# One product for the high and the low activations in the feature-major units of a one-core layer kernel

## The chip, the cores and the metric

The kernel runs on one core of a Trainium2 chip. The metric is the device time of one execution in microseconds; lower is better. The time before is 1656.69 us, the median of three runs (1654.15 to 1658.95).

A core has five engines that matter here, each with an instruction queue of its own that it works off in order: TensorE (PE in the profile; its weight loads are listed apart as PEld), VectorE (DVE), ScalarE (ACT), GpSimd (POOL) and SyncE (SP), which issues the weight transfers. They wait for each other by semaphores.

## The reference

One decoder layer on 256 tokens of width 2048, in float32:

```python
u = rmsnorm(h, w1)
qkv_A, z_A, b_A, a_A, q_B, k_B, v_B, g_B, gate_A, gate_B = split(u @ w_in)
q, k, v = silu(causal_conv(qkv_A, width 4))       # mixer A
o_A = gated_delta_rule(l2norm(q), l2norm(k), v, sigmoid(b_A), decay(a_A))
o_B = retention(rotary(q_B), rotary(k_B), v_B)    # mixer B
h = h + (sigmoid(gate_A) * o_A + sigmoid(gate_B) * o_B) @ w_out
h = h + SwiGLU(rmsnorm(h, w2))
return rmsnorm(h, wf)
```

Both mixers have 8 heads with 128 key and 256 value columns. The delta rule and the retention go by chunks of tokens.

## The kernel before

**Precision.** Float32 accuracy is had from TensorE's faster 32-bit type by splitting: a value is a high part (rounded to that type) and a low part (the rest). A product of two split values takes three products: high by high, high by low, low by high. The activations `u` are split once, into `uh` and `ul`. Each weight tile of 128 x 2048 is split when it arrives: ScalarE writes `hi` (L169), VectorE writes `lo` as raw minus `hi` (L170).

**Units.** The projections are cut into units of one weight tile. In a *feature-major* unit the weights are the stationary operand: 128 output features, 16 slices of 128 input features, 256 tokens as the moving columns. For each slice, PE multiplies `hi` with the high activations (L235) and then the same `hi` with the low ones (L236), each 128x256; when all slices are done come 16 products of `lo` with the high ones (L238). All 48 go into one half of a PSUM bank, 128x256. In a *token-major* unit the activations are stationary and the weights move, 512 columns at a time (L286, L287, L291); some of these are computed as Strassen sums of half tiles (`Z_t`, L378 to L382).

There are 64 feature-major units. Each of the four blocks (two heads each) has eight for the convolution of mixer A (k0, k1, q0, q1, v00, v01, v10, v11; functions `conv_unit`) and four for the rotary part of mixer B (r0 to r3; `rot_evac`); then 16 units multiply the merged mixers by `w_out` (`wo_evac`). After them the FFN runs; its products are token- or group-wise and are not feature-major.

**What follows a unit.** A convolution unit is read by VectorE from PSUM times `rstd_b` into `cb` (L501); ScalarE scales it by the first tap (L504); VectorE adds three taps (L506); ScalarE takes the sigmoid (L509); VectorE multiplies the two (L511) into `kT`, `qT` or `vt`. A rotary unit is read from PSUM by VectorE three times (L798 to L800) and summed into `rot` (L801). A `w_out` unit is added to `hT` by VectorE (L1096).

**Order.** Units follow lists written by hand; Strassen units are woven between the units of a block. `run_units` runs a unit and then what was put off to it: `after(n, fn)` runs `fn` when n more units have been issued. The weights run ahead of the units through 3 raw, 2 `hi` and 2 `lo` buffers. Within that program order a scheduler decides the order of each engine's queue. PSUM has eight banks: four for sums (which the first units also use), two for units (`pp`), two for everything else (`mx`); so with `pp` alone, a unit gets the bank of the unit two before it. In the first block, the function `decay` computes the decays from a small product `pab` through ScalarE's sigmoid, exp and log (L1012 to L1020), `gt` on VectorE (L1024) and two small PE products `pe` and `pd` (L1029 to L1040).

`ACT_TABLE_LOAD` in a row is ScalarE loading a table before a function that the loaded table lacks. Copies and scalings need none.

Of the kernel before, what the change touches and what calls it, by code (L numbers as in the profile page):

```python
# [66 lines left out]
def kernel(  # L67
# [156 lines left out]
            for fn in events.pop(done[0], []):  # L224
                fn()

    def feature_major(src, nk, ah, al, name, evac):
        o = []

        def begin():  # L230
            o.append(ps_unit(f"ps_{name}")[:, :S])

        def products(hi, lo, k0, k1):
            for k in range(k0, k1):
                PE.matmul(o[0], hi[:, k * P:(k + 1) * P], ah[:, k, :], start=(k == 0), stop=False)  # L235
                PE.matmul(o[0], hi[:, k * P:(k + 1) * P], al[:, k, :], start=False, stop=False)  # L236
            for k in range(k0, k1):
                PE.matmul(o[0], lo[:, k * P:(k + 1) * P], ah[:, k, :], start=False, stop=(k == nk - 1))  # L238

        def compute(hi, lo):  # L240
            begin()
            g = nk if unit[0] != 3 or not first[0] else nk // Q2
            for k in range(0, nk, g):
                products(hi, lo, k, k + g)
            evac(o[0])
        compute.steps = begin, products, lambda: evac(o[0])
        units.append((src, nk * P, name, compute))

    def start_pair(before):

        c = [units[i][3].steps for i in range(2)]
        for i in range(2):
            fetched.append(wtile("raw", units[i][2], F32))
            parts.append((wtile("hi", units[i][2]), wtile("lo", units[i][2])))
            loaded.append(parts[i])
        for q in range(4):
            before(q)
            r = slice(512 * q, 512 * q + 512)
            for i in range(2):
# [13 lines left out]
        units[1] = units[1][:3] + (both,)  # L273

    def token_major(src, uh, ul, name, evac, bank):
        pst = []
# [165 lines left out]
            PE.matmul(pb[:, c * P:(c + 1) * P], ones, dg[:, c], start=True, stop=True)  # L442
        return pb

    uh = act.tile([P, KT, S], F32R, tag="a0", name="uh")
    ul = act.tile([P, KT, S], F32R, tag="a1", name="ul")
    xs = act.tile([P, KT, S], F32, tag="a2", name="xs")
    xq = act.tile([P, KT, S], F32, tag="a3", name="xq")
    mm = {}
# [5 lines left out]
    def t1(name, n=S):  # L455
        return mixp.tile([P, 260], F32, tag="t1", name=name, bufs=T1B)[:, :n]
# [21 lines left out]
    def z_tiles(name):  # L478
        return mt([P, 5, S], "Z", f"Z_{name}"), t1(f"s1_{name}")

    def flat(t):
        return t.rearrange("p a b -> p (a b)")

    def v4(ps, n=P):
        return ps[:, :4 * n].rearrange("p (a b) -> p a b", a=4)

# [3 lines left out]
    def conv_unit(b, i, name, dst, then):  # L490

        def evac(o):
            if done[0] <= HOLD + 1:
                after(HOLD + 1 - done[0], lambda: finish(o))
            else:
                finish(o)

        def finish(o):
            cb = t1(f"cb_{name}", S + 3)
            G.memset(cb[:, 0:3], 0.0)  # L500
            V.tensor_tensor(out=cb[:, 3:], in0=o, in1=rstd_b, op=ALU.mult)  # L501
            cv = t1(f"cv_{name}")
            w = cvw[:, b * 8 + i]
            A_.activation(cv, cb[:, 0:S], AF.Copy, scale=w[:, 0:1])  # L504
            for j in range(1, 4):
                V.scalar_tensor_tensor(out=cv, in0=cb[:, j:j + S], scalar=w[:, j:j + 1], in1=cv,  # L506
                                       op0=ALU.mult, op1=ALU.add)
            sg = t1(f"sg_{name}")
            A_.activation(sg, cv, AF.Sigmoid)  # L509
            d = dst()  # L510
            V.tensor_tensor(out=d, in0=cv, in1=sg, op=ALU.mult)  # L511
            then(d)
        feature_major(wqk[b * 12 + i], KT, uh, ul, name, evac)

    def new_parts(i):

        mm[i] = act.tile([P, 2, KT // 2, S], F32R, tag=f"a{2 + i}", name=f"m{i}")

    def merged_parts(b, j):
        k = 4 * (b % 2) + 2 * j  # L520
        return flat(mm[b // 2][:, 0, k:k + 2]), flat(mm[b // 2][:, 1, k:k + 2])

    class Merged:
        def __init__(self, part):
            self.part = part

        def __getitem__(self, r):
            _, k, t = r
            return mm[k // (KT // 2)][:, self.part, k % (KT // 2), t]

    def split_rest():

        new_parts(1)
        if "wait" in mm:
            for j in range(2):
                hv, lv = merged_parts(2, j)
                w = mm["wait"][:, 512 * j:512 * j + 512]
# [20 lines left out]
    def block(b):  # L558
# [231 lines left out]


        def rot_evac(i):
            def evac(o):
                if i == 0:
                    T["rot"] = mt([P, 4, S], "rv", f"rot_{b}")
                ra = t1(f"ra_{b}_{i}")
                rb_ = t1(f"rb_{b}_{i}")
                V.tensor_tensor(out=ra, in0=o, in1=cosr, op=ALU.mult)  # L798
                V.tensor_tensor(out=rb_[0:64], in0=o[64:128], in1=sinr[64:128], op=ALU.mult)
                V.tensor_tensor(out=rb_[64:128], in0=o[0:64], in1=sinr[0:64], op=ALU.mult)  # L800
                V.tensor_tensor(out=T["rot"][:, i], in0=ra, in1=rb_, op=ALU.add)  # L801
# [87 lines left out]
        def merge(j):  # L889
# [163 lines left out]
    done[0] = unit[0] = 0  # L1053
    first[0] = False

    mh, ml = Merged(0), Merged(1)


    with tc.tile_pool(name="ffn", bufs=1) as ffn:
        for tag in WBUFS:  # L1060
# [9 lines left out]
        hh = act.tile([P, KT, S], F32R, tag="a0", name="hh")  # L1070
        hl = act.tile([P, KT, S], F32R, tag="a1", name="hl")
# [301 lines left out]
```

## Time and profile before

| | before |
|---|---|
| median of three runs | 1656.69 us |
| profiled execution | 1654.24 us |
| its span in the trace | 1652.5 us |
| PE busy | 1626.6 us, 98% |
| DVE busy | 1292.9 us, 78% |
| ACT busy | 821.6 us, 50% |
| chain that ended last | PE 91%, DVE 4%, DMA 3% |

The profile is one execution. Busy time counts the instructions of an engine; matmuls are pipelined, so the records of neighbouring ones overlap, and the pace of PE is read from start to start, not from a record's duration. The chain is followed back from the last instruction to what released each step.

### The profile page before, as it was taken

How to read it: one execution, taken by the hardware profiler on the slowest of the kernel's cores; microseconds unless marked ns; L12 is line 12 of the kernel's file. 1: busy time of each engine (PE TensorE's matmuls, PEld its weight loads, DVE VectorE, ACT ScalarE, POOL GpSimd, SP SyncE). 2: the span in 40 equal slices, each digit the busy share in tenths (PEclk: the TensorE clock that was granted, in tenths of full speed). 3: DMA queues.
4: the chain of work that ended last, by engine and by line, in shares of the span. 5: the costliest groups of instructions: out<-in, count | busy, mean ns of one | idle time of the engine just before them, and what ended most of it. 6: DMA issues, size and time to landing. Idle time of an engine off the chain costs nothing.

```text
span 1652.5 us, 26750 instructions
## 1 busy us (share of the span) xinstructions
PE 1626.6 (98%) x11226; PEld 1459.9 (88%) x11226; DVE 1292.9 (78%) x1648; ACT 821.6 (50%) x815; POOL 35.0 (2%) x64
## 2 busy tenths in 40 slices
PE   7999999999999999999999999999999999999998
PEld 6987899988998889988899888888888888888887
DVE  7797468887897878776766877889987998878764
ACT  5664444445553555444565645444554445545442
POOL 0000000000000000000000100000000000000000
PEclk9999999999999999999999999999999999999999
DMA  7545454455545555355574556456674565755751
GB/s 270 179 154 171 153 194 135 155 186 171 208 141 192 166 176 200 126 174 167 199 290 142 168 196 221 144 188 192 203 230 151 191 193 170 246 181 182 233 200 52
DMA packets 90458, 301.11 MB, mean 182 GB/s; under 512 B 6752, under 2 KB 11104, under 8 KB 74592
## 3 DMA queue, kind: packets, MB, share of 16 engines
q1 hardware_dynamic: 88896, 295.31, 53.7%
q10 hardware_dynamic: 1440, 4.08, 0.7%
q8 instruction: 88, 1.44, 0.3%
q14 instruction: 34, 0.28, 0.0%
HBM read 297.27 MB, written 2.10 MB: 181 GB/s over the span
## 4 chain that ended last, share of the span: by engine, by line
PE 91%; DVE 4%; DMA 3%; ACT 1%; issue 1%; SPq 0%; POOL 0%; ACTq 0%; DVEq 0%
PE ps_wd L315 12%; PE pst_su L362 7%; PE ps_t L286 7%; PE ps_t L291 7%; PE ps_t L287 7%; PE ps_wu L315 7%; PE ps_wg L315 6%; PE pst_t L362 6%; PE pst_sg L362 5%; PE ps_v L236 2%; PE ps_v L235 2%; PE ps_r L235 2%; PE ps_v L238 2%; PE ps_r L236 2%; PE ps_wo L235 2%; PE ps_wo L236 2%
## 5 line engine op out<-in xcount | busy, mean ns | idle before, releaser
L169 ACT ACTIVATE hi_t<-raw_t 128x2048 fp32r<-128x2048 f32 (+1 forms) x100 | 183.1, 1831 | 204.6 <-PE ps_t L287 104.6
L170 DVE TENSOR_TENSOR lo_t<-raw_t,hi_t 128x2048 fp32r<-128x2048 f32 (+1 forms) x100 | 217.8, 2182 | 60.7 <-ACT hi_t L169 42.0
L286 PE MATMUL ps_t<-hi_t,uh 128*128 128x512 f32 x480 | 190.7, 397 | 0.5 <-DVE gs L874 0.5
L287 PE MATMUL ps_t<-hi_t,ul 128*128 128x512 f32 x480 | 188.6, 393 | 0.0
L315 PE MATMUL ps_wd<-hi_wd,f 128*128 128x512 f32 x704 | 170.6, 391 | 1.0 <-DVE f L1183 1.0
L315 PEld LDWEIGHTS ps_wd<-hi_wd,f 128*128 128x128 f32 x704 | 129.9, 188 | 27.0 <-DVE f L1183 1.2
L169 ACT ACTIVATE hi_sg<-raw_sg 128x1792 fp32r<-128x1792 f32 x48 | 81.6, 1702 | 118.5 <-DVE raw_sg L189 68.9
L169 ACT ACTIVATE hi_su<-raw_su 128x1792 fp32r<-128x1792 f32 x48 | 81.6, 1699 | 85.2 <-DVE raw_su L189 47.7
L291 PE MATMUL ps_t<-lo_t,uh 128*128 128x512 f32 x480 | 123.5, 395 | 0.0
L170 DVE TENSOR_TENSOR lo_su<-raw_su,hi_su 128x1792 fp32r<-128x1792 f32 x48 | 97.0, 2022 | 32.4 <-ACT hi_su L169 15.3
L169 ACT ACTIVATE hi_wd<-raw_wd 128x2048 fp32r<-128x2048 f32 x44 | 84.3, 1915 | 68.5 <-PE ps_wd L315 27.8
L170 DVE TENSOR_TENSOR lo_wd<-raw_wd,hi_wd 128x2048 fp32r<-128x2048 f32 x44 | 100.6, 2286 | 19.8 <-ACT hi_wd L169 19.7
L170 DVE TENSOR_TENSOR lo_sg<-raw_sg,hi_sg 128x1792 fp32r<-128x1792 f32 x48 | 96.9, 2021 | 16.8 <-PE ps_wd L315 7.8
L286 PEld LDWEIGHTS ps_t<-hi_t,uh 128*128 128x128 f32 x480 | 90.2, 188 | 19.1 <-PE pst_t L362 0.9
L287 PEld LDWEIGHTS ps_t<-hi_t,ul 128*128 128x128 f32 x480 | 90.2, 188 | 17.7
L291 PEld LDWEIGHTS ps_t<-lo_t,uh 128*128 128x128 f32 x480 | 88.9, 188 | 18.1
L315 PE MATMUL ps_wd<-lo_wd,f 128*128 128x512 f32 x352 | 88.6, 391 | 3.4 <-DVE lo_wd L170 3.4
L315 PEld LDWEIGHTS ps_wd<-lo_wd,f 128*128 128x128 f32 x352 | 64.8, 188 | 16.8 <-DVE lo_wd L170 4.0
L235 PE MATMUL ps_v<-uh,hi_v 128*128 128x256 f32 x256 | 63.6, 286 | 0.6 <-DVE cb_v L501 0.6
L235 PE MATMUL ps_wo<-m,hi_wo 128*128 128x256 f32 x256 | 62.5, 285 | 0.8 <-ACT gs L872 0.8
L236 PE MATMUL ps_v<-ul,hi_v 128*128 128x256 f32 x256 | 63.2, 285 | 0.0
L315 PE MATMUL ps_wg<-hi_wg,hh 128*128 128x512 f32 x160 | 62.8, 392 | 0.3 <-ACT hi_wg L169 0.3
(346 smaller groups left out, 3889.5 us busy)
## 6 DMA issues: line engine op xcount, KB each, us to landing
raw_t<-in_wtm_dram SPq DMA_DIRECT2D x60, 1024.0 KB, 4.9
raw_wd<-in_wdown_dram SPq DMA_DIRECT2D x44, 1024.0 KB, 5.1
raw_sg<-in_wst_dram SPq DMA_DIRECT2D x48, 512.0 KB, 3.5
raw_su<-in_wst_dram SPq DMA_DIRECT2D x48, 512.0 KB, 3.6
raw_t<-in_wsm_dram SPq DMA_DIRECT2D x40, 512.0 KB, 3.6
raw_wg<-in_wgate_dram SPq DMA_DIRECT2D x20, 1024.0 KB, 5.1
raw_wu<-in_wup_dram SPq DMA_DIRECT2D x20, 1024.0 KB, 5.1
raw_v<-in_wqk_dram SPq DMA_DIRECT2D x16, 1024.0 KB, 4.9
```

The lines of the kernel that those rows point to most:

```text
L169: ia = A_.activation(hi[:, r], w[:, r], AF.Copy)
L170: iv = V.tensor_tensor(out=lo[:, r], in0=w[:, r], in1=hi[:, r].bitcast(F32), op=ALU.subtract)
L235: PE.matmul(o[0], hi[:, k * P:(k + 1) * P], ah[:, k, :], start=(k == 0), stop=False)
L236: PE.matmul(o[0], hi[:, k * P:(k + 1) * P], al[:, k, :], start=False, stop=False)
L238: PE.matmul(o[0], lo[:, k * P:(k + 1) * P], ah[:, k, :], start=False, stop=(k == nk - 1))
L286: PE.matmul(pst[c], uh[:, k, c * P:(c + 1) * P], w, start=(k == 0), stop=False)
L287: PE.matmul(pst[c], ul[:, k, c * P:(c + 1) * P], w, start=False, stop=False)
L291: PE.matmul(pst[c], uh[:, k, c * P:(c + 1) * P], lo[:, j * 512:(j + 1) * 512], start=False, stop=(k == KT - 1))
L315: PE.matmul(pst[c], u[:, k, c * P:(c + 1) * P], w[:, k], start=(start and k == 0 and q == 0), stop=(stop and k == 3))
L362: PE.matmul(T[bank][:, half * S:(half + 1) * S], op(j), w[:, slot * 256:(slot + 1) * 256], start=(j == 0 and w is hi and h and half == 0), ...
```

## The change

The high and the low activations are laid out next to each other for every slice (`u2`, `m`, `h2`), so that one product of 512 columns multiplies `hi` with both. A feature-major unit now takes a whole PSUM bank: the first half holds high by high (and the low weights are added there), the second half holds high by low. The two halves are added after the unit:

- convolution: ScalarE copies the second half to `cl`; one unit later VectorE adds the first half to it, then multiplies by `rstd_b`. Silu is one ScalarE instruction, in place of sigmoid and VectorE's product.
- rotary: ScalarE copies the second half; one unit later VectorE adds the first and turns from SBUF.
- `w_out`: VectorE adds both halves to `hT` one after the other.

```diff
+    def feature_major(src, nk, a, name, evac, joined=False):
 ...
-            o.append(ps_unit(f"ps_{name}")[:, :S])
+            o.append(ps_unit(f"ps_{name}")[:, :2 * S if joined else S])
 ...
             for k in range(k0, k1):
-                PE.matmul(o[0], hi[:, k * P:(k + 1) * P], ah[:, k, :], start=(k == 0), stop=False)
-                PE.matmul(o[0], hi[:, k * P:(k + 1) * P], al[:, k, :], start=False, stop=False)
+                w = hi[:, k * P:(k + 1) * P]
+                if joined:
+                    PE.matmul(o[0], w, flat(a(k)), start=(k == 0), stop=(k == nk - 1), skip_group_check=True)
+                    continue
 ...
             for k in range(k0, k1):
-                PE.matmul(o[0], lo[:, k * P:(k + 1) * P], ah[:, k, :], start=False, stop=(k == nk - 1))
+                PE.matmul(o[0][:, :S], lo[:, k * P:(k + 1) * P], a(k)[:, 0], start=False, stop=(k == nk - 1),
+                          skip_group_check=joined)
 ...
-    uh = act.tile([P, KT, S], F32R, tag="a0", name="uh")
-    ul = act.tile([P, KT, S], F32R, tag="a1", name="ul")
+    u2 = act.tile([P, KT, 2, S], F32R, tag="a0", name="u2")
+    uh, ul = u2[:, :, 0], u2[:, :, 1]
 ...
         def finish(o):
+            cl = t1(f"cl_{name}")
+            A_.activation(cl, o[:, S:], AF.Copy)
+            after(1, lambda: taps(o, cl))
+
+        def taps(o, cl):
             cb = t1(f"cb_{name}", S + 3)
             G.memset(cb[:, 0:3], 0.0)
-            V.tensor_tensor(out=cb[:, 3:], in0=o, in1=rstd_b, op=ALU.mult)
+            V.tensor_tensor(out=cl, in0=o[:, :S], in1=cl, op=ALU.add)
+            V.tensor_tensor(out=cb[:, 3:], in0=cl, in1=rstd_b, op=ALU.mult)
 ...
-            sg = t1(f"sg_{name}")
-            A_.activation(sg, cv, AF.Sigmoid)
             d = dst()
-            V.tensor_tensor(out=d, in0=cv, in1=sg, op=ALU.mult)
+            A_.activation(d, cv, AF.Silu)
 ...
-            def evac(o):
+            def evac(ps):
+                o = t1(f"ro_{b}_{i}")
+                A_.activation(o, ps[:, S:], AF.Copy)
+                after(1, lambda: turn(ps, o))
+
+            def turn(ps, o):
+                V.tensor_tensor(out=o, in0=ps[:, :S], in1=o, op=ALU.add)
 ...
             def evac(o):
-                V.tensor_tensor(out=hT[:, f], in0=o, in1=hT[:, f], op=ALU.add)
+                for i in range(2):
+                    V.tensor_tensor(out=hT[:, f], in0=o[:, i * S:(i + 1) * S], in1=hT[:, f], op=ALU.add)
```

SP's queue of transfers reads the same in both kernels. On the other engines the change moves instructions; three places follow, each first before and then after.

PE in block 0, around the decay's products `pe` and `pd`. `ps_r`/`ps_v` are units of the rotary part and of the values; the number behind a name only tells tiles apart. Before, `pe` stands in the second rotary unit, behind 5 of its products:

```order
L238 MATMUL ps_r_903<-uh,lo_r_778 128x256 x16
L235 MATMUL ps_r_972<-uh,hi_r_899 128x256
L236 MATMUL ps_r_972<-ul,hi_r_899 128x256
L235 MATMUL ps_r_972<-uh,hi_r_899 128x256
L236 MATMUL ps_r_972<-ul,hi_r_899 128x256
L235 MATMUL ps_r_972<-uh,hi_r_899 128x256
L1029 MATMUL pe<-gt,cs 128x16
L1030 MATMUL pe<-gt,cs 128x16
L1040 MATMUL pd_660<-cs,lg_661 128x128 x4
```

After, it stands behind 10 joined products of the last value unit, 1.7 units further up:

```order
L239 MATMUL ps_v_664<-u_93,hi_v_608 128x512 x10
L1038 MATMUL pe<-gt,cs 128x16
L1039 MATMUL pe<-gt,cs 128x16
L239 MATMUL ps_v_664<-u_93,hi_v_608 128x512 x5
L1049 MATMUL pd_558<-cs,lg_559 128x128 x4
L1049 MATMUL pd_570<-cs,lg_571 128x128 x4
L239 MATMUL ps_v_664<-u_93,hi_v_608 128x512
L244 MATMUL ps_v_664<-u_93,lo_v_609 128x256 x15
L1049 MATMUL pd_582<-cs,lg_583 128x128 x4
L244 MATMUL ps_v_664<-u_93,lo_v_609 128x256
```

The products of the decay are moved up in PE's order; what they need has to be there earlier.

ACT at the same place, which makes `tln`, from which `gt` comes. Before:

```order
L1012 ACTIVATE beta<-ab 128x16
L169 ACTIVATE hi_r_899<-raw_r_775 128x2048
L1016 ACTIVATE tabs<-av 128x16
L509 ACTIVATE sg_v_562<-cv_v_557 128x256
L1018 ACT_TABLE_LOAD
L1018 ACTIVATE tex<-tabs 128x16
L1020 ACT_TABLE_LOAD
L1020 ACTIVATE tln<-tex 128x16
L504 ACTIVATE cv_v_645<-cb_v_642,cvw 128x256
```

After:

```order
L169 ACTIVATE hi_v_608<-raw_v_500 128x2048
L1027 ACT_TABLE_LOAD
L1027 ACTIVATE tex<-tabs 128x16
L522 ACT_TABLE_LOAD
L522 ACTIVATE kT_405<-cv_k_411 128x256
L1029 ACT_TABLE_LOAD
L1029 ACTIVATE tln<-tex 128x16
L522 ACT_TABLE_LOAD
L522 ACTIVATE qT_426<-cv_q_421 128x256
L517 ACTIVATE cv_q_473<-cb_q_469,cvw 128x256
L507 ACTIVATE cl_v_539<-ps_v_506 128x256
L517 ACTIVATE cv_v_545<-cb_v_541,cvw 128x256
```

Silu (L522) and the decay's exp and log (L1027, L1029) alternate, each with a table load, and the copy `cl` of a unit stands behind them.

DVE at the start of block 2, where the units k0 and k1 are read; `lo_q` are the splits for q0 and q1, two units on from each. Before, k0 is read (L501) ahead of q0's split, and k1 behind q1's:

```order
L501 TENSOR_TENSOR cb_k_4309<-ps_k_4260,rstd_b 128x256
L170 TENSOR_TENSOR lo_q_4342<-raw_q_4254,hi_q_4341 128x2048
L382 TENSOR_TENSOR Z_t_4237<-pst_t_1_3722,Z_t_4237 128x512
L506 SCALAR_TENSOR_TENSOR cv_k_4312<-cb_k_4309,cvw,cv_k_4312 128x256 x3
L170 TENSOR_TENSOR lo_q_4408<-raw_q_4339,hi_q_4407 128x2048
L501 TENSOR_TENSOR cb_k_4394<-ps_k_4345,rstd_b 128x256
```

After, k1 is read (L513) behind q1's split again, and q0 behind that of v00, two units on:

```order
L170 TENSOR_TENSOR lo_q_4023<-raw_q_3968,hi_q_4022 128x2048
L513 TENSOR_TENSOR cl_k_4007<-ps_k_3974,cl_k_4007 128x256
L887 TENSOR_TENSOR oa_3491<-oa_3491,ob_3317 128x512
L519 SCALAR_TENSOR_TENSOR cv_k_4013<-cb_k_4009,cvw,cv_k_4013 128x256
L514 TENSOR_TENSOR cb_k_4061<-cl_k_4007,rstd_b 128x256
L170 TENSOR_TENSOR lo_v_4074<-raw_v_4020,hi_v_4073 128x2048
L513 TENSOR_TENSOR cl_q_4059<-ps_q_4026,cl_q_4059 128x256
```

The instruction that frees a unit's PSUM bank stands behind one 128x2048 split, which before held for some of the units only.

## Rows read from the trace of the kernel before

**Rows 1.** The page, its first part: busy time, share of the span, instructions.
```profile
PE 1626.6 (98%) x11226; PEld 1459.9 (88%) x11226; DVE 1292.9 (78%) x1648; ACT 821.6 (50%) x815; POOL 35.0 (2%) x64
```

**Rows 2.** The page, the chain that ended last, by engine.
```profile
PE 91%; DVE 4%; DMA 3%; ACT 1%; issue 1%; SPq 0%; POOL 0%; ACTq 0%; DVEq 0%
```

**Rows 3.** Timeline of PE, a k unit: start, duration, engine, line, operation, count.
```profile
425.81 2.08 PE L238 MATMUL ps_k<-uh,lo_k 128*128 128x256 f32 x16
427.73 0.28 PE L235 MATMUL ps_k<-uh,hi_k 128*128 128x256 f32 x1
427.85 0.28 PE L236 MATMUL ps_k<-ul,hi_k 128*128 128x256 f32 x1
```

**Rows 4.** Timeline of PE, a token-major unit: first and last of 16 products in a row.
```profile
813.31 0.39 PE L286 MATMUL ps_t<-hi_t,uh 128*128 128x512 f32 x1
...
816.71 0.39 PE L287 MATMUL ps_t<-hi_t,ul 128*128 128x512 f32 x1
```

**Rows 5.** Groups by line, L235: count; min/median/max ns; first and last start.
```profile
L235 PE MATMUL ps_v<-uh,hi_v x256: 278/283/388, 42.8 to 667.8; 128*128 128x256 f32 x128
...
L235 PE MATMUL ps_k<-uh,hi_k x128: 277/283/579, 7.8 to 629.2; 128*128 128x256 f32 x128
```

**Rows 6.** Waits of PE: line, releaser, us in total, times, longest.
```profile
PE ss_n L986 <- DVE sx L982: 3.9, 2, 3.2
```

**Rows 7.** DVE by windows: us, its length, DVE busy (count), PEclk, DMA share, GB/s.
```profile
421.00:466.00 45.00, 41.06 (x65) 1.00 0.52 178
466.00:513.00 47.00, 41.68 (x71) 1.00 0.47 158
...
819.00:914.00 95.00, 58.81 (x67) 1.00 0.58 206
```

**Rows 8.** Groups by line on DVE: the split, reads of units, attention product.
```profile
L170 DVE TENSOR_TENSOR lo_v<-raw_v,hi_v x16: 2280/2292/2294, 38.7 to 657.1; 128x2048 fp32r<-128x2048 f32 x16
...
L501 DVE TENSOR_TENSOR cb_k<-ps_k,rstd_b x8: 416/420/427, 38.4 to 633.9; 128x256 f32<-128x256 f32 x8
...
L1096 DVE TENSOR_TENSOR hT<-ps_wo,hT x16: 412/424/426, 839.7 to 916.5; 128x256 f32<-128x256 f32 x16
...
L766 DVE SCALAR_TENSOR_TENSOR at<-pq,cf,Ei x16: 340/343/347, 105.1 to 666.6; 128x128 f32<-128x128 f32 x16
...
L647 DVE STREAM_TRANSPOSE MTc<-Mc x16: 300/306/315, 115.3 to 710.5; 128x128 f32<-128x128 f32 x16
```

**Rows 9.** ACT, by line: a table load, a PSUM copy, the first tap.
```profile
L509 ACT ACT_TABLE_LOAD  x3: 1283/1283/1283, 43.1 to 84.8; - x3
...
L376 ACT ACTIVATE s_t<-pst_t x5: 357/363/370, 336.4 to 798.4; 128x256 f32<-128x256 f32 x5
...
L504 ACT ACTIVATE cv_v<-cb_v,cvw x16: 490/504/513, 60.5 to 676.8; 128x256 f32<-128x256 f32 x16
```

**Rows 10.** Timeline of ACT around a table load.
```profile
41.14 1.92 ACT L169 ACTIVATE hi_v<-raw_v 128x2048 fp32r<-128x2048 f32 x1 [1.72 <-PE ps_q L236]
43.08 1.28 ACT L509 ACT_TABLE_LOAD   x1
44.37 0.42 ACT L509 ACTIVATE sg_k<-cv_k 128x256 f32<-128x256 f32 x1
```

**Rows 11.** Timeline of the decay in block 0, all engines.
```profile
66.29 0.28 PE L235 MATMUL ps_r<-uh,hi_r 128*128 128x256 f32 x1
...
69.74 0.22 ACT L1020 ACTIVATE tln<-tex 128x16 f32<-128x16 f32 x1
...
70.20 0.17 DVE L1024 SCALAR_TENSOR_TENSOR gt<-sp,ea 128x16 f32<-128x16 f32 x1
...
72.65 0.29 PE L1029 MATMUL pe<-gt,cs 128*128 128x16 f32 x2
```

**Rows 12.** Timeline where the `w_out` units begin, all engines.
```profile
824.68 0.82 PE L897 MATMUL pmt<-cs,oa 128*128 128x128 f32 x6
825.21 0.60 ACT L905 ACTIVATE m<-pmt 128x512 fp32r<-128x512 f32 x1 [5.00 <-PE pmt L897]
```

More of the change, by code (lines that the diff above doesn't have):

```diff
@@ L225, in flush @@
                 fn()
-    def feature_major(src, nk, ah, al, name, evac):
+    def feature_major(src, nk, a, name, evac, joined=False):
         o = []
         def begin():
-            o.append(ps_unit(f"ps_{name}")[:, :S])
+            o.append(ps_unit(f"ps_{name}")[:, :2 * S if joined else S])
         def products(hi, lo, k0, k1):
             for k in range(k0, k1):
-                PE.matmul(o[0], hi[:, k * P:(k + 1) * P], ah[:, k, :], start=(k == 0), stop=False)
-                PE.matmul(o[0], hi[:, k * P:(k + 1) * P], al[:, k, :], start=False, stop=False)
+                w = hi[:, k * P:(k + 1) * P]
+                if joined:
+                    PE.matmul(o[0], w, flat(a(k)), start=(k == 0), stop=(k == nk - 1), skip_group_check=True)
+                    continue
+                PE.matmul(o[0], w, a(k)[:, 0], start=(k == 0), stop=False)
+                PE.matmul(o[0], w, a(k)[:, 1], start=False, stop=False)
             for k in range(k0, k1):
-                PE.matmul(o[0], lo[:, k * P:(k + 1) * P], ah[:, k, :], start=False, stop=(k == nk - 1))
+                PE.matmul(o[0][:, :S], lo[:, k * P:(k + 1) * P], a(k)[:, 0], start=False, stop=(k == nk - 1),
+                          skip_group_check=joined)
         def compute(hi, lo):
@@ L273, in start_pair, with flat @@
         units[1] = units[1][:3] + (both,)
+    def flat(t):
+        return t.rearrange("p a b -> p (a b)")
     def token_major(src, uh, ul, name, evac, bank):
@@ L479, in z_tiles @@
         return mt([P, 5, S], "Z", f"Z_{name}"), t1(f"s1_{name}")
-    def flat(t):
-        return t.rearrange("p a b -> p (a b)")
     def v4(ps, n=P):
@@ L507, in finish @@
                                        op0=ALU.mult, op1=ALU.add)
-            sg = t1(f"sg_{name}")
-            A_.activation(sg, cv, AF.Sigmoid)
             d = dst()
-            V.tensor_tensor(out=d, in0=cv, in1=sg, op=ALU.mult)
+            A_.activation(d, cv, AF.Silu)
             then(d)
-        feature_major(wqk[b * 12 + i], KT, uh, ul, name, evac)
+        feature_major(wqk[b * 12 + i], KT, lambda k: u2[:, k], name, evac, joined=True)
     def new_parts(i):
-        mm[i] = act.tile([P, 2, KT // 2, S], F32R, tag=f"a{2 + i}", name=f"m{i}")
+        mm[i] = act.tile([P, KT // 2, 2, S], F32R, tag=f"a{2 + i}", name=f"m{i}")
     def merged_parts(b, j):
         k = 4 * (b % 2) + 2 * j
[L521 to L529, printed above, removed]
+        return mm[b // 2][:, k:k + 2, 0], mm[b // 2][:, k:k + 2, 1]
     def split_rest():
@@ L536, in split_rest @@
                 hv, lv = merged_parts(2, j)
-                w = mm["wait"][:, 512 * j:512 * j + 512]
+                w = halves(mm["wait"][:, 512 * j:512 * j + 512])
                 A_.activation(hv, w, AF.Copy)
@@ L904, in merge @@
             hv, lv = merged_parts(b, j)
-            A_.activation(hv, ps, AF.Copy)
-            V.tensor_tensor(out=lv, in0=ps, in1=hv.bitcast(F32), op=ALU.subtract)
+            A_.activation(hv, halves(ps), AF.Copy)
+            V.tensor_tensor(out=lv, in0=halves(ps), in1=hv.bitcast(F32), op=ALU.subtract)
         n = f"{b}"
@@ L917, in block @@
         for i in range(4):
-            feature_major(wqk[b * 12 + 8 + i], KT, uh, ul, f"r{i}" + n, rot_evac(i))
+            feature_major(wqk[b * 12 + 8 + i], KT, lambda k: u2[:, k], f"r{i}" + n, rot_evac(i), joined=True)
         sides = []
@@ L1054 @@
     first[0] = False
-    mh, ml = Merged(0), Merged(1)
     with tc.tile_pool(name="ffn", bufs=1) as ffn:
@@ L1069 @@
         nc.scalar.dma_start(wfs, wf)
-        hh = act.tile([P, KT, S], F32R, tag="a0", name="hh")
-        hl = act.tile([P, KT, S], F32R, tag="a1", name="hl")
+        h2 = act.tile([P, KT, 2, S], F32R, tag="a0", name="h2")
+        hh, hl = h2[:, :, 0], h2[:, :, 1]
         sh = act.tile([P, KT // 2, 4, P], F32R, tag="a2", name="sh")
@@ L1249 @@
         for f in range(KT):
-            feature_major(wout[f], KT, mh, ml, f"wo{f}", wo_evac(f))
+            feature_major(wout[f], KT, lambda k: mm[k // 8][:, k % 8], f"wo{f}", wo_evac(f), joined=True)
         for mains, sides in ROW:
```

## The prediction

> **What bounds the kernel now.** I read the page's first part, then the chain of waits, then PE's pace on the timeline, and last the engines that feed PE. PE is busy for 1626.6 of 1652.5 us [rows 1], and 91% of the chain that ended last is PE [rows 2]. The largest wait of PE on one releaser is 3.9 us [rows 6]. So a product that leaves PE's queue shortens the time almost one for one, as long as the engines that empty PSUM and split weights keep their place behind PE. The granted clock is 1.00 in the stretches shown [rows 7], the 2.4 GHz level, so the pace read there holds for them.
>
> **The pace of PE.** The first product of the next unit starts 0.120 us before the second (427.73, 427.85), and 16 products of the low weights take 1.92 us, also 0.120 each [rows 3]. A product of 512 columns has a pace of (816.71 − 813.31)/15 = 0.2267 us [rows 4]. A joined product replaces two of 256 columns: 0.240 − 0.2267 = 0.0133 us. L235 runs 256 times each for v, r and `w_out` and 128 times each for k and q (v and k stand for the two counts) [rows 5]: 1024 joined products, 13.6 us. A unit becomes 16 × 0.0133 = 0.21 us shorter: 5.76 us (32 × 0.120 + 1.92) becomes 5.55. Not all of it shows: from the first k product at 7.8 to the first v product at 42.8 [rows 5] lie 35.0 us, but four units at pace take 23.0, so PE is starved there. For two and a half of these units I count nothing (0.5 us). Gain: **13.1 us**.
>
> TensorE's price for many small products bears on this first term. Rows 3 and 4 give 0.120 and 0.2267 us, so 13 ns more than the columns alone at 2.4 GHz (106.7 and 213.3). The Trainium skill ("TensorE: Matmul & The Clock Gate", section "Wait — 56ns, not 53.3ns?") gives about 2.5 ns per product beyond N/2.4 GHz; by it, two 256-column products cost 218.3 ns and one of 512 costs 215.8, so the joining would save 2.6 us in all, not 13.6. The trace does not agree: the paces of rows 3 and 4 are of this kernel at the full clock, and I go by them.
>
> **What VectorE gains and loses.** Convolution (32 units): the new add L513 replaces the product after the sigmoid, one 128x256 two-input operation for another, so nothing. Rotary: 16 adds; `w_out`: 16 adds. By 0.42 us each (L501 and L1096) [rows 8], 32 × 0.42 = 13.4 us on an engine that is busy for 58.81 of 95 us in the `w_out` stretch [rows 7]: with 6.7 more it is at 65.5 of 92, and hidden. In the rotary stretch 466 to 513 it has 41.68 of 47 [rows 7]; four adds make 43.4 of 46.2, 94%. In the convolution stretch 421 to 466 it has 41.06 of 45; the same work in 1.5 us less is 94%. PE's cover there is thin, which is the place to look.
>
> **What ScalarE gains.** 48 copies of a half bank at 0.363 us (L376) [rows 9] are 17.4 us; sigmoid becomes silu one for one (silu doesn't occur in the trace: between a copy and twice a sigmoid's 0.42 us [rows 10] it changes the sum by under 14 us on this engine). Table loads rise from 9 to 19 in the order: 10 × 1.283 us [rows 9] = 12.8. In all 821.6 + 30 of some 1645: 52%, hidden on the average. A load costs its 1.28 us and no more: `hi_v` ends at 43.06, the load starts at 43.08, ends at 44.36, the sigmoid starts at 44.37 [rows 10]. The Trainium skill ("ScalarE: Activation LUTs", section "What ACT_TABLE_LOAD costs") adds a drain of about 1.38 us to each switch; these rows show none, and only the next term would change by it: 3.3 would become about 9 us.
>
> **Three places where PE gets a new wait.**
>
> 1. *The decay of block 0.* Before, `gt` starts at 70.20 and `pe` at 72.65 [rows 11]: 2.3 us of slack. Now `pe` stands 1.7 units further up. The second rotary unit's start, 66.29 + 5.76 [rows 11], puts the last value unit before at 60.5; with five shorter units it starts at 59.4, and `pe` is due 10 products later, at 61.7. ScalarE's row: the split for that unit waits for a buffer until the joined products of v01 end (v01 starts two units before the last, at 48.3; 16 × 0.2267 later is 51.9), 1.92 us [rows 10]; then load and exp 1.5, load and silu 1.7, load and log 1.5: `tln` at 58.5. But `gt` now stands behind VectorE's add of `cl_v`, whose copy stands behind load and silu 1.7, a first tap 0.5 [rows 9] and 0.36 for itself: 61.1. The add takes 0.42 and `gt` 0.17: 61.7, and with the gaps between engines some 62.1, 0.4 late. Then VectorE's queue sets the pace: four `lg` rows against five products, 0.5 late; four more with a tap between, 0.9 late; and the third `pd` behind a split of 2.29 [rows 8], 1.5 late. Sum **3.3 us**; 0 if the copies come as early as the order assumes, 7 if each step is late by another tap or load.
> 2. *The start of `w_out`.* The last transposes (`pmt` x6, 824.68) are split by ScalarE at 825.21 for 0.60 us [rows 12] and then by VectorE. Before, the products with the high parts needed only ScalarE's; a joined one needs VectorE's low part too, of about 0.65 us, directly behind the transposes: 1.15 us after their end instead of about 0. Term **1.2 us** (0 to 2).
> 3. *The PSUM banks of blocks 1 to 3.* A unit's bank is free only when VectorE has added its first half, one unit later in program order and behind the split of the unit after next: 2.29 + 0.42 [rows 8] after the unit's end, about 2.7, where the bank is needed 5.55 after. The cover is 2.8 us. At 94% busy VectorE is sometimes later than that. I take **1.5 us**; nothing if the queue keeps pace, and up to 21 as worked out under the rivals.
>
> The convolution's result comes a unit later to what reads it; the block's chains of small products start from lists in units and find the same distance, and the merge of block 3 has the token-major units between. I cost that at nothing; if a chain's rows came late, PE would stand about one tap or add, 0.4 us, at each of three blocks.
>
> **Sum.** The profiled execution took 1654.24 us, 1.7 around its span, 0.15% under the median of the runs shown (1656.69). 1654.24 − 13.1 + 3.3 + 1.2 + 1.5 = 1647.1 us. As runs of before lie up to 4 us above their profile, I write 1648.
>
> **Rivals.**
> - *PE stays fed.* Terms 1 to 3 vanish since the queues were laid out with these dependences: 1654.2 − 13.1 = 1641. For it: the largest wait of before is small, and VectorE's rows are in the order in which they become ready. Against: `gt` behind an add that hangs on three table loads.
> - *VectorE eats the gain.* In the convolution and rotary stretches it runs at 94%, so it cannot follow units that are 0.21 us shorter: of the 48 units of the blocks, the 36 of blocks 1 to 3 give their 7.7 us back, and block 0's term stays: 1654.2 − 13.1 + 7.7 + 4.5 = 1653. For it: rows 7. Against: 6% of 90 us is still 5 us of idle time per block.
> - *The fixed price per product* (the rule above): a gain of 2.6 us against the 6.0 of the three terms, 1657.6.
> - *The bank held by VectorE's queue* (slower). When block work stands before the add, four `at` at 0.343 and four `MTc` at 0.306 [rows 8] and three taps of about 0.48, 4.0 us, the bank is free 6.7 us after its unit, 1.2 late, and PE stands. From VectorE 2.8 us late on, each such unit costs; with 6 of 12 units in each of three blocks, 18 × 1.2 = 21 us: 1654.2 − 13.1 + 21 + 4.5 = 1667. It decides from 11 units of the 36. For it: DVE is above 90% and reads now stand behind the splits. Against: such clumps are short in the order.
>
> **Chances.** The forecast 0.46, PE stays fed 0.19, VectorE eats the gain 0.17, the price per product 0.06, the bank 0.12. About 0.3%, 5 us, can be told from no change: faster is below 1651.7. The forecast and the second case lie below but for a small part (0.01); with it, 0.64 faster. The third and fourth lie within, plus that part: 0.24 same. The last is slower: 0.12. The range 1640 to 1658 takes in the first four; the likeliest case's own is 1643 to 1652 by the bounds of its terms.
>
> **What the profile after would show.** Right: L239 at a pace of 0.227 us and L244 at 0.120; PE busy about 13 us shorter; a wait of PE for `gt`, `lg` near 62 us; one of about 1 us on the last `m` where `w_out` starts; small waits of joined products in blocks 1 to 3 on L513 or the rotary add. Wrong: a pace of 0.237 or more for L239 (price), waits of a microsecond on ps_k, ps_q, ps_v or ps_r that repeat from unit to unit (bank), DVE idle near zero in 421 to 513 (VectorE), or no waits at the two places (PE stays fed).

## The result and the profile after

The changed kernel takes 1644.51 us, the median of four runs (1644.22 to 1646.91), against 1656.97 before: ratio 0.9927, 95% interval 0.9916 to 0.9939. In a later series it was 1645.92 against 1658.88, again 0.9927 (0.9914 to 0.9939). It is 12.5 us faster; forecast were 1648 and 7 to 9 us, and 1641 for the case that PE stays fed. The time lies between the two. Executions of one kernel differ by some us with TensorE's granted clock: of 25 executions of the kernel before, the eight at a mean clock of 0.998 took 1653.9 to 1655.1 us, the others, at 0.995 to 0.997, 1656.0 to 1659.6; the profile of before is one at 0.998, that of the changed kernel is at 0.995.

The page of the changed kernel, its first part and its chain by engine, answers to [rows 1, 2]:

```profile
PE 1617.0 (98%) x10202; PEld 1406.1 (86%) x10202; DVE 1304.3 (79%) x1680; ACT 845.6 (51%) x873; POOL 34.6 (2%) x64
...
PE 91%; DVE 3%; DMA 1%; ACT 1%; issue 0%; POOL 0%; ACTq 0%; DVEq 0%
```

PE has exactly 1024 products less. The pace answers to [rows 3, 4]; PE's timeline in the same k units of block 2:

```profile
424.18 3.82 PE L239 MATMUL ps_k<-u,hi_k 128*128 128x512 f32 x16
427.83 2.08 PE L244 MATMUL ps_k<-u,lo_k 128*128 128x256 f32 x16
429.75 3.82 PE L239 MATMUL ps_q<-u,hi_q 128*128 128x512 f32 x16
```

From 424.18 to 427.83 are 16 joined products, 0.228 us each; the 16 low ones take 1.92 as before. A unit takes 5.57 us instead of 5.76; 5.55 was forecast.

The waits of PE in the changed kernel (line, releaser, us in total, times, longest) answer to [rows 6]:

```profile
PE ss_n L995 <- DVE sx L991: 3.0, 1, 3.0
...
PE pe L1038 <- DVE gt L1033: 1.1, 1, 1.1
PE ps_wo L239 <- DVE m L915: 1.1, 1, 1.1
...
PE ps_t L296 <- ACT vr L827: 0.4, 1, 0.4
...
PE pd L1049 <- DVE lg L1048: 0.3, 1, 0.3
```

Four waits are new. Three are those that were forecast by place: `gt`, `lg` and `m`. The fourth was not forecast: 0.4 us in block 1, for ScalarE's read (`vr`) of a token-major unit's bank. None is on the bank of a feature-major unit.

Where the time came from, measured from the first product of a stage to the first of the next, in us (the first stage from the first k product, the FFN to the start of PE's last product; blocks 0 and 1 together, since the boundary between them shifts with the order of their rows):

| kernel | blocks 0, 1 | block 2 | block 3 | `w_out` | FFN |
|---|---|---|---|---|---|
| before | 413.7 | 198.4 | 199.8 | 95.8 | 731.0 |
| after | 410.9 | 194.7 | 196.9 | 94.2 | 732.0 |
| after, second series | 411.8 | 194.7 | 196.9 | 94.2 | 736.1 |
| joined, sigmoid | 411.4 | 199.0 | 205.4 | 94.2 | 732.3 |
| joined, product on GpSimd | 415.8 | 200.9 | 198.6 | 94.3 | 735.9 |
| joined, read at once | 425.1 | 205.6 | 202.8 | 94.2 | 735.8 |
| joined, banks held | 419.7 | 202.1 | 201.1 | 94.2 | 732.9 |
| joined, product read by nobody | 410.8 | 195.0 | 197.1 | 94.2 | 735.5 |
| silu alone | 416.7 | 197.9 | 199.5 | 95.8 | 732.7 |
| late read alone | 414.8 | 199.5 | 199.0 | 95.8 | 732.6 |

Blocks 2 and 3 and `w_out` repeat to 0.02 us between the two executions of the changed kernel, while blocks 0 and 1 differ by 0.9 us and the FFN by 4.1. So a stage's length in blocks 2 and 3 tells more than the whole time of one execution.

### The profile page after: what moved, and what is told of

Its sections match the earlier page's. It is cut to its first block, busy times and chain, and to the rows that moved or that the text cites. A ratio compares the mean times of both kernels' runs of the same rounds, so it can differ in the third digit from the quotient of the medians.

```text
span 1642.4 us, 24810 instructions
## 1 busy us (share of the span) xinstructions
PE 1617.0 (98%) x10202; PEld 1406.1 (86%) x10202; DVE 1304.3 (79%) x1680; ACT 845.6 (51%) x873; POOL 34.6 (2%) x64
## 4 chain that ended last, share of the span: by engine, by line
PE 91%; DVE 3%; DMA 1%; ACT 1%; issue 0%; POOL 0%; ACTq 0%; DVEq 0%
PE ps_wd L325 14%; PE pst_su L372 7%; PE ps_t L296 7%; PE ps_t L297 7%; PE ps_t L301 7%; PE ps_wu L325 7%; PE pst_t L372 6%; PE ps_wg L325 6%; PE pst_sg L372 6%; PE ps_r L239 4%; PE ps_wo L239 4%; PE ps_v L239 3%; PE ps_wo L244 2%; PE ps_r L244 2%; PE ps_v L244 1%; PE ps_q L239 1%
## 5 line engine op out<-in xcount | busy, mean ns | idle before, releaser
L296 PE MATMUL ps_t<-hi_t,u 128*128 128x512 f32 x480 | 192.0, 400 | 0.4 <-ACT vr L827 0.4
L297 PE MATMUL ps_t<-hi_t,u 128*128 128x512 f32 x480 | 188.3, 392 | 0.0
L301 PE MATMUL ps_t<-lo_t,u 128*128 128x512 f32 x480 | 121.6, 392 | 0.0
L296 PEld LDWEIGHTS ps_t<-hi_t,u 128*128 128x128 f32 x480 | 90.2, 188 | 18.7 <-ACT vr L827 0.6
L301 PEld LDWEIGHTS ps_t<-lo_t,u 128*128 128x128 f32 x480 | 89.7, 188 | 18.7
L297 PEld LDWEIGHTS ps_t<-hi_t,u 128*128 128x128 f32 x480 | 90.2, 188 | 17.7
L325 PE MATMUL ps_wg<-hi_wg,h 128*128 128x512 f32 x320 | 78.9, 392 | 0.3 <-ACT hi_wg L169 0.3
L325 PE MATMUL ps_wu<-hi_wu,h 128*128 128x512 f32 x320 | 76.5, 390 | 0.0
L325 PEld LDWEIGHTS ps_wu<-hi_wu,h 128*128 128x128 f32 x320 | 59.2, 188 | 11.7
L325 PEld LDWEIGHTS ps_wg<-hi_wg,h 128*128 128x128 f32 x320 | 58.3, 188 | 11.6 <-ACT hi_wg L169 0.8
```

Of the source, the lines that this page charges most:

```text
L296: PE.matmul(pst[c], uh[:, k, c * P:(c + 1) * P], w, start=(k == 0), stop=False)
L297: PE.matmul(pst[c], ul[:, k, c * P:(c + 1) * P], w, start=False, stop=False)
L301: PE.matmul(pst[c], uh[:, k, c * P:(c + 1) * P], lo[:, j * 512:(j + 1) * 512], start=False, stop=(k == KT - 1))
L325: PE.matmul(pst[c], u[:, k, c * P:(c + 1) * P], w[:, k], start=(start and k == 0 and q == 0), stop=(stop and k == 3))
```

## The experiments

**Parts of the join.** Joined products in the output projection alone, everything else as before. Of the edit, the convolution's units; the rotary ones likewise, and what follows a unit is put back to sigmoid, product and a read at once:

```diff
-        feature_major(wqk[b * 12 + i], KT, lambda k: u2[:, k], name, evac, joined=True)
+        feature_major(wqk[b * 12 + i], KT, lambda k: u2[:, k], name, evac)
 ...
```

> Joined products in the 16 units of the output projection alone; convolution and rotary units as before (two products of 256 columns, sigmoid, read at once). Theory: 256 joined products save 0.0133 us each, 3.4 us, less a wait of 1.1 us for VectorE's low part of the last merged slices: about 2.3 us, ratio 0.9986, and a pace of 0.227 us in these units alone. Rival (a fixed price of 2.5 ns per product): 0.7 us saved and 1.1 lost, ratio 1.000.

Measured: ratio 0.9997 (0.9988 to 1.0006). The interval takes in the rival's 1.000 and ends just above the theory's 0.9986, so the whole time does not decide; the stage does. `w_out` took 94.2 instead of 95.8 us, 1.6 and not 2.3, with the wait of 1.1 on `m`; the rival had it 0.4 us longer. Of 16 × 0.19 = 3.0 us less 1.1, 0.3 us is not accounted for.

The complement, joined products in the blocks alone:

```diff
-            feature_major(wout[f], KT, lambda k: mm[k // 8][:, k % 8], f"wo{f}", wo_evac(f), joined=True)
+            feature_major(wout[f], KT, lambda k: mm[k // 8][:, k % 8], f"wo{f}", wo_evac(f))
 ...
```

(with one add to `hT` in `wo_evac` again).

> Joined products in the 48 convolution and rotary units alone; the output projection as before (two products of 256 columns, one add). Theory: 768 joined products save 10.2 us, of which 0.5 lie in the starved start and 1.4 go to the decay's waits in block 0: about 8.3 us, ratio 0.995, and no wait of a microsecond where the output projection starts. Rival (fixed price): 2 us saved and 1.4 lost, ratio 1.000.

Measured: 0.9948 (0.9931 to 0.9965), as expected; no wait on `m`. Blocks 2 and 3 take 194.7 and 196.9 us and `w_out` 95.8: the two parts add up. The fixed price per product is out, here and by the pace.

**Silu.** The kernel before with silu, nothing joined:

```diff
-            A_.activation(sg, cv, AF.Sigmoid)
-            V.tensor_tensor(out=d, in0=cv, in1=sg, op=ALU.mult)
+            A_.activation(d, cv, AF.Silu)
```

> The kernel before with silu on ScalarE in place of sigmoid and VectorE's product, nothing joined. Theory: VectorE is 13.4 us less busy, ScalarE loads 19 tables instead of 9, and PE's queue keeps its length: ratio 1.000 within 0.001. Rival (silu carries part of the gain by relieving VectorE): ratio 0.997 or less. Other rival (the table loads by themselves delay the decay of block 0): up to 3 us slower, 1.002, with a wait of PE on gt.

Measured: 1.0007 (0.9997 to 1.0016): no gain. The stages show two effects: blocks 0 and 1 are 3.0 us longer (a wait of 1.7 us of PE for `gt`, behind table loads, and then a granted clock of 0.57 from 63 to 67 us with PE fully busy), blocks 2 and 3 are 0.5 and 0.3 shorter.

The changed kernel with that edit undone, all units joined:

> The changed kernel with the convolution's sigmoid on ScalarE and the product on VectorE again, as before; all units stay joined and read one unit later. Theory (the gain is the joined products' pace and nothing else): VectorE has 32 products more, 13.4 us busy in all, hidden; 11 table loads instead of 19; the ratio to before stays at 0.993 within 0.001. Rival (VectorE is nearly the bound in the convolution stretches, and silu is what makes room for the add): eight products of 0.42 us per block on an engine 94% busy there make 101%; 1 to 3 us lost in each of four blocks, ratio 0.995 to 0.999, and waits of PE on units' PSUM banks.

Measured: 1.0017 (1.0006 to 1.0028). The whole gain is gone: 1659.27 us. The rival had the direction but neither the size nor the place: 4.3 and 8.5 us are lost in blocks 2 and 3, and not on banks. The largest wait of PE in block 2, and what stood in VectorE's row (the sigmoid first, on ScalarE):

```profile
PE pss_q L572 <- DVE qT L524: 2.7, 1, 2.7
```

```profile
460.59 0.40 ACT L522 ACTIVATE sg_q<-cv_q 128x256 f32<-128x256 f32 x1
```

```profile
461.68 2.02 DVE L170 TENSOR_TENSOR lo_t<-raw_t,hi_t 128x1792 fp32r<-128x1792 f32 x1
463.61 0.42 DVE L524 TENSOR_TENSOR qT<-cv_q,sg_q 128x256 f32<-128x256 f32 x1
```

The sigmoid ended at 461.0, and the product started 2.6 us later, behind a split. The waits of PE in block 3, from 618 us to the start of `w_out` (columns as above):

```profile
PE pv L790 <- DVE vt L524: 4.9, 1, 4.9
PE ps_wo L239 <- ACT gs L883: 0.8, 1, 0.8
PE pP L643 <- DVE Mc L651: 0.4, 1, 0.4
```

ScalarE's and VectorE's timelines of that place:

```profile
691.83 0.40 ACT L522 ACTIVATE sg_v<-cv_v 128x256 f32<-128x256 f32 x1
```

```profile
692.43 0.69 DVE L187 TENSOR_TENSOR raw_t<-raw_t 128x512 f32<-128x512 f32 x1 [1.25 <-DMA raw_t<-in_wsm_dram]
693.04 0.29 DVE L644 TENSOR_TENSOR Pc<-pP,cs 128x128 f32<-128x128 f32 x1
693.24 2.28 DVE L170 TENSOR_TENSOR lo_t<-raw_t,hi_t 128x2048 fp32r<-128x2048 f32 x1
695.44 0.42 DVE L188 TENSOR_TENSOR raw_t<-raw_t 128x256 f32<-128x256 f32 x1
695.78 0.42 DVE L524 TENSOR_TENSOR vt<-cv_v,sg_v 128x256 f32<-128x256 f32 x1
```

The sigmoid was there at 692.2. The product, 0.42 us of work, started 3.6 us later, since in VectorE's row stand first a weight sum, late by a wait of 1.25 us for a transfer, and a split of 2.28. PE's row had `pv` next. Then it got worse; the granted clock around it, by windows (us, length, PE busy, PEclk, DMA share, GB/s):

```profile
691.00:697.00 6.00, 1.09 (x35) 0.80 0.24 67
697.00:703.00 6.00, 6.00 (x18) 0.63 0.39 161
703.00:709.00 6.00, 6.00 (x35) 1.00 0.15 22
```

After this stop PE worked 6 us at a mean of 0.63, between the two levels of 1.2 and 2.4 GHz: 13 joined products took 5.33 us instead of 3.1.

**Load or place?** That run has both more work on VectorE and the last step of the convolution in its queue. The next one has the work without the place:

```diff
             A_.activation(d, cv, AF.Silu)
+            V.tensor_tensor(out=cv, in0=cv, in1=cv, op=ALU.mult)
```

> The changed kernel (silu) with one more product of 0.42 us on VectorE per convolution unit, in place and read by nobody, behind silu: VectorE's queue has the same number of products as in the run with sigmoid (ratio 1.002), but what PE reads is made by ScalarE. Theory (the loss there came from kT, qT and vt being made in VectorE's queue, behind splits): ratio 0.993 to 0.996, no wait of pv of several us. Rival (VectorE's load in the convolution stretches is the bound, wherever the product stands): ratio 1.000 or more, with waits of PE on what VectorE makes.

Measured: 0.9923 (0.9909 to 0.9936), like the changed kernel; no wait of `pv`. The load is that of the run with sigmoid, by the pages of the two (first the sigmoid's, then this one's):

```profile
PE 1621.8 (98%) x10202; PEld 1409.0 (85%) x10202; DVE 1315.5 (79%) x1712; ACT 836.1 (50%) x865; POOL 43.1 (3%) x64
```

```profile
PE 1619.2 (98%) x10202; PEld 1407.0 (85%) x10202; DVE 1312.6 (80%) x1712; ACT 846.5 (51%) x874; POOL 35.1 (2%) x64
```

1712 instructions and about 1314 us each, and ratios of 1.0017 and 0.9923. So VectorE's load is not the cause. That the place is, is read from the trace at the two long waits, 2.7 and 4.9 us, each for a product behind a split; it is not isolated, since the scheduler lays out PE's row anew for each kernel: the last `pv` of block 3 is the 637th product of its block in the run with sigmoid and the 560th here.

The product on GpSimd, out of VectorE's queue:

```diff
-            V.tensor_tensor(out=d, in0=cv, in1=sg, op=ALU.mult)
+            G.tensor_tensor(out=d, in0=cv, in1=sg, op=ALU.mult)
```

> The changed kernel with sigmoid on ScalarE and the product of the convolution on GpSimd, so that it stands in no queue of VectorE. Theory (the last run with this product on VectorE, at ratio 1.002, lost its gain because the product waited in VectorE's queue behind splits and weight sums): the gain comes back, ratio 0.993 to 0.995, the wait of pv for vt is gone or under a microsecond. Rival (what costs is the longer way from the taps to kT, qT and vt, one more engine and instruction): ratio above 0.998, since GpSimd's product is not shorter than VectorE's 0.42 us, with waits of pv and pss_q on GpSimd.

Measured: 1.0022 (1.0012 to 1.0032). The theory's expectation failed, and the run doesn't tell the two apart as meant, for GpSimd is far slower than was assumed (line, count, min/median/max ns):

```profile
L524 POOL TENSOR_TENSOR vt<-cv_v,sg_v x16: 733/2506/2573, 78.8 to 692.8; 128x256 f32<-128x256 f32 x16
```

For `kT` and `qT` the medians are 930 and 745 ns. The largest single wait of `pv` for `vt` is 1.0 us now instead of 4.9, and block 3 took 198.6 us instead of 205.4; but six smaller new waits came, and blocks 0 to 2 took 6.3 us more than in that run. The trace shows what makes the products long. Nineteen of the 32 were started while VectorE worked on a split, and each of them ended 0.6 us after that split's end (one 0.9): 18 took 2.2 to 2.8 us, one 1.1. The other 13 took 0.73 to 0.75 us, one 1.1. The last `vt`, one of the long ones, and the split that had started 0.09 us before it:

```profile
692.76 2.52 POOL L524 TENSOR_TENSOR vt<-cv_v,sg_v 128x256 f32<-128x256 f32 x1 [3.87 <-ACT sg_v L522]
```

```profile
692.67 2.03 DVE L170 TENSOR_TENSOR lo_t<-raw_t,hi_t 128x1792 fp32r<-128x1792 f32 x1 [1.22 <-PE ps_r L244]
```

So a product on GpSimd is out of VectorE's queue, but not out of the way of its splits.

**The read one unit later.** Undone:

```diff
-            after(1, lambda: taps(o, cl))
+            taps(o, cl)
```

(and the same for the rotary units).

> The changed kernel with the first half of a convolution or rotary unit added as soon as the unit ends, in program order, instead of one unit later. Theory (what decides is that no instruction on VectorE stands in PE's way for long, and the later add is one that fits VectorE's queue behind a split): VectorE then waits for ScalarE's copy with its splits queued behind it; PE loses a few microseconds on products that need them or on the block's small chains, ratio 0.994 to 0.997, against 0.993. Rival (the read one unit later only holds the banks longer and is worth nothing): ratio 0.993 or a little less.

Measured: 1.0125 (1.0107 to 1.0144), 1677.87 us. The direction was expected, the size was not by far. PE's largest new waits:

```profile
PE pv L788 <- ACT vt L522: 4.7, 2, 2.5
PE ps_r L239 <- DVE cl_v L513: 4.5, 3, 2.2
...
PE pP L641 <- DVE Mc L633: 3.7, 1, 3.7
```

They are on results of several kinds, banks among them: with the adds earlier, other rows of VectorE stand later than PE's row needs them. Which of the moved rows started it was not singled out. PE's waits in the blocks sum to some 20 us of the 33; and the mean granted clock is 0.988, not 0.995.

By itself the later read is no gain; in the kernel before:

> The kernel before with the convolution and rotary units read one unit later, nothing joined, sigmoid and product as before. Theory (the later read only fits the order to a longer way from the unit to its result; by itself it moves the results of the convolution a unit back): ratio 0.999 to 1.004. Rival (the later read by itself gives VectorE's queue room and carries part of the gain): ratio 0.997 or less.

Measured: 1.0011 (1.0002 to 1.0020), as the theory had it.

**The banks.** 15 more operations on VectorE (0.286 us each, 4.3 us) ahead of one add in each of blocks 1 to 3:

```diff
+            if b > 0 and i == 4:
+                for _ in range(15):
+                    V.tensor_scalar(out=cl, in0=cl, scalar1=1.0, scalar2=None, op0=ALU.mult)
             V.tensor_tensor(out=cl, in0=o[:, :S], in1=cl, op=ALU.add)
```

> The changed kernel with 15 more operations on VectorE (the second half times one, in place, 128x256) ahead of the add of the first value unit in each of blocks 1 to 3: that unit's bank is held some 5 us longer. Theory (the cover for a late add is about 2.8 us): the unit two on waits for the bank, a wait of PE of 1.5 to 4 us per block on ps_v, 5 to 12 us in all. Rival (the banks have more cover than that, or VectorE's idle time takes it up): no wait on ps_v, under 3 us longer in all.

One execution: 1665.99 us. Both expectations failed: blocks 1 to 3 lost some 20 us, but the unit two on did not wait. The waits:

```profile
PE pv L791 <- ACT vt L525: 3.8, 3, 2.6
...
PE pM L651 <- DVE Pc L645: 1.8, 1, 1.8
PE pst_t L372 <- ACT hi_t L169: 1.7, 1, 1.7
PE ps_r L239 <- DVE cl_v L516: 1.3, 1, 1.3
```

The run does not test the cover of 2.8 us. The scheduler wove the 15 operations between other rows, in block 1 from 257.4 to 272.6 us, so the held unit's add ended at 275.5 and not 4.3 us later than in the changed kernel (257.3). And the unit two on started at 259.8, before that add, so it has another bank; the held unit's bank went to a Strassen sum (`pst_t`), and PE waited 0.6 us for it. The other wait on a bank, 1.3 us, is on a later unit's. The longest wait, 2.6 us of `pv` in block 2, is for the held unit's own result: when VectorE's add is late here, the convolution's result costs more than the banks.

**Towards a better one.** The decay of block 0 one unit later (`after(2, ...)` for `after(1, ...)`), and the first two `w_out` units in two parts:

```diff
+            if name in ("wo0", "wo1"):
+                g = 12
             for k in range(0, nk, g):
-                products(hi, lo, k, k + g)
+                products(hi, lo, k, min(nk, k + g))
 ...
```

> The changed kernel with the decay of block 0 begun one unit later and the first two units of the output projection in two parts (12 slices with their low weights, then the last 4). Theory (PE's new waits at these two places are real and can be covered): the waits of 1.1 and 0.3 us on gt and lg and of 1.1 us on the last merged low part go, 2.5 us, ratio 0.9912 against 0.9927. Rival (the later decay meets the start of block 0's small chains, or PE is held elsewhere soon after): ratio 0.9927 or higher.

Beside it the changed kernel again:

> The changed kernel as it is, for a closer ratio beside the next run: 0.9927 within 0.001.

Measured: 0.9923 (0.9910 to 0.9937) against 0.9927 for the changed kernel: not told apart. `w_out` is 1.4 us shorter (92.8), its wait gone; the decay's waits moved and grew, as the rival had it, to 1.8 us on `gt` and 1.5 on ScalarE's `Ei`, and blocks 0 and 1 took 413.8 us.

Last, sigmoid in block 0 alone with the two-part `w_out` units:

```diff
+            if b == 0:
+                sg = t1(f"sg_{name}")
+                A_.activation(sg, cv, AF.Sigmoid)
+                V.tensor_tensor(out=d, in0=cv, in1=sg, op=ALU.mult)
+            else:
+                A_.activation(d, cv, AF.Silu)
```

> The changed kernel with sigmoid and VectorE's product in block 0 alone (silu in blocks 1 to 3), and the first two units of the output projection in two parts. Theory (in block 0, where the decay alternates exp and log with the convolution's function, the table loads of silu eat the joined products' gain; in blocks 1 to 3 they cost nothing): block 0 takes some 213.8 us as in the run with sigmoid instead of 215.9, the output projection 92.8 instead of 94.2, 3.5 us in all, ratio 0.9906. Rival (block 0's gain there came from another order of its units that this kernel does not have): block 0 at 215 to 217 us, ratio 0.9919.

Measured: 0.9928 (0.9914 to 0.9941). The waits of the decay are gone, but a new one takes their place near the end of block 0 (PE's timeline; the bracket is the idle time and its releaser):

```profile
200.57 0.70 PE L710 MATMUL px<-y,MT 128*128 128x256 f32 x2 [1.83 <-DVE y L726]
```

Blocks 0 and 1 together took 411.6 us, no less than 410.9 to 411.8. Block 0 alone had looked shorter in the run with sigmoid because block 1's first product came earlier in the order, ahead of eight token-major products (1.8 us). No version beats the changed kernel measurably.

## Why the prediction was right, and where not

**The pace and the gain of 13.1 us: right, a little less.** A unit gained 0.19 us, not 0.21; 61.5 units make 11.7. The profiled executions differ by 1654.2 − 1644.2 = 10.0 us: blocks 0 and 1 gave 2.8, blocks 2 and 3 3.7 and 2.9, `w_out` 1.6, the FFN, whose products are the same, took 1.0 more (from 1285 to 1290 us, after PE had waited 2.2 us, the changed kernel's granted clock was 0.66, and the profile of before has no such stretch in its FFN). The medians differ by 12.5, since the profile of before is one of its short executions. PE is busy for 9.6 us less, where 13 were forecast.

**ScalarE's cost is hidden: right, but for 0.4 us.** It is 24.0 us busier, 30 were forecast; the 0.4 us is the new wait for `vr`. Silu's table loads show no drain; ScalarE's timeline of the changed kernel answers to [rows 10]:

```profile
58.37 1.28 ACT L1029 ACT_TABLE_LOAD   x1
59.67 0.21 ACT L1029 ACTIVATE tln<-tex 128x16 f32<-128x16 f32 x1
59.90 1.28 ACT L522 ACT_TABLE_LOAD   x1
61.19 0.42 ACT L522 ACTIVATE qT<-cv_q 128x256 f32<-128x256 f32 x1
61.52 0.49 ACT L517 ACTIVATE cv_q<-cb_q,cvw 128x256 f32<-128x256 f32 x1
61.92 0.36 ACT L507 ACTIVATE cl_v<-ps_v 128x256 f32<-128x256 f32 x1
```

Each function starts 1.29 to 1.30 us after its load's start. By these rows the 1.38 us of drain that the Trainium skill gives ("ScalarE: Activation LUTs", section "What ACT_TABLE_LOAD costs") is not there. The term that would have been about 9 us with it, by the prediction's estimate from that page, is 1.4.

**The decay: place and chain right, size too large.** `tln` was forecast for the end of ScalarE's row at 58.5 and came at 59.9. The sum had the split start when its buffer comes free, at 51.9; it started at 53.20, since a table load and `beta` stand ahead of it, which the sum left out:

```profile
51.68 1.28 ACT L1021 ACT_TABLE_LOAD   x1
52.97 0.21 ACT L1021 ACTIVATE beta<-ab 128x16 f32<-128x16 f32 x1
...
53.20 1.90 ACT L169 ACTIVATE hi_v<-raw_v 128x2048 fp32r<-128x2048 f32 x1
```

PE's and VectorE's rows, which answer to [rows 11]:

```profile
62.45 0.42 DVE L513 TENSOR_TENSOR cl_v<-ps_v,cl_v 128x256 f32<-128x256 f32 x1
62.78 0.17 DVE L1033 SCALAR_TENSOR_TENSOR gt<-sp,ea 128x16 f32<-128x16 f32 x1
```

```profile
63.00 0.40 PE L1038 MATMUL pe<-gt,cs 128*128 128x16 f32 x2 [1.10 <-DVE gt L1033]
```

`gt` stood behind the add of `cl_v`, as worked out. `pe` waited 1.1 us, not 0.4. The steps after it failed: "VectorE's queue sets the pace" was priced at 0.5 + 0.9 + 1.5 us, and PE waited 0.3 for all of them. Term 1.4 instead of 3.3.

**`w_out`: right.** 1.1 us on `m`, 1.2 forecast; it answers to [rows 12].

**The banks: too dear.** 1.5 us was taken, nothing was measured. The cover is thinner than the 2.8 us of the sum, though: the closest of blocks 1 to 3 are the units k1 of blocks 2 and 3. In block 2 the read of k1 ends at 434.28, and q1, two units on, takes the bank at 435.53, 1.25 us later:

```profile
433.86 0.42 DVE L513 TENSOR_TENSOR cl_k<-ps_k,cl_k 128x256 f32<-128x256 f32 x1
```

```profile
435.53 3.82 PE L239 MATMUL ps_q<-u,hi_q 128*128 128x512 f32 x16
```

The sum had every unit's bank go to the unit two on. For the first value unit of each of these blocks that is not so, as the run with the added operations showed.

**What the sum did not have.** Blocks 2 and 3 gained 6.6 us where the shorter units give 24 × 0.19 = 4.6. Two waits of before are gone in block 2, 0.6 us on a unit's bank (`cb_v`) and one of the two on `gs`, 0.3:

```profile
PE ps_v L235 <- DVE cb_v L501: 0.6, 1, 0.6
PE ps_t L286 <- DVE gs L874: 0.5, 2, 0.3
```

The first is gone with silu alone too, which gives 0.8 in the two blocks. Some 1 us is open: from start to start it lies mostly in the `pv` products, 0.9 us less for the same sixteen, which stand elsewhere in PE's row; why was not singled out.

**The step that hid the most: "Convolution: ... one two-input operation for another, so nothing".** As a count it is right, and it left out where the product stands. With the product kept on VectorE the gain is lost, at the same load at which it is kept when nobody reads the product. So the rival "VectorE eats the gain" named a real danger by the wrong measure. In the stretches that answer to [rows 7], VectorE of the changed kernel is busy for 92 and 94% (94 was forecast for both), and the gain is there:

```profile
418.00:463.00 45.00, 41.35 (x72) 1.00 0.48 164
463.00:510.00 47.00, 44.31 (x71) 1.00 0.51 169
```

In these runs the share did not decide; by the two long waits, what stood in the queue in front of the result that PE reads next did.

Silu and the later read are each worth nothing or less alone (1.0007, 1.0011), the join without either loses everything (1.0017, 1.0125), and all three give 0.9927. The prediction read the changed order only where it looked for a wait. It did not see that the order with all three is worth 15 and 33 us against the others; that it fits was not worked out, and to that extent the forecast had luck.

## What to carry to other kernels

Where one product can take two operands that share the stationary weights, its pace tells the gain, and the gain is real if the engine is the bound. Then the work is in what empties the banks: put the last step of a chain that PE reads on an engine whose queue is short at that place and which does the step as fast (on GpSimd it was no gain), and price a moved step by what stands in front of it, not by its own duration or its engine's busy share alone.

When stages repeat to hundredths of a microsecond and the rest of the program scatters by several, compare stages; and beware of a boundary that the order itself moves.

## What was not expected of the hardware

- A stop of 4.9 us of PE cost more than itself: the granted clock was 0.80 in the 6 us around it and 0.63 in the 6 us after, when PE was fully busy again; then 1.00. In the run that read at once, a stop of 3.7 us was followed by 6 us at 0.65.
- GpSimd's 128x256 product took 0.73 us at best and 2.5 at the median for `vt`, against 0.42 on VectorE. The long ones are those started during a split of VectorE: they ended 0.6 us after it. Five that had started before a split took no longer for it (0.74 to 0.75 us).
- Two runs of the same kernel agree in blocks 2 and 3 to 0.02 us and differ by 4.1 us in the FFN.
